# Second layer of a float32 encoder on one core: all heads' probabilities turned through VectorE and DMA, three output blocks in step, the last heads' holds dropped

## The chip, the core and the metric

The kernel runs on one NeuronCore of one Trainium2 chip. The metric is device time in microseconds (us), lower is better. Before the change the median of three runs is 1994.85 us (1994.55 to 1995.7).

## The reference

A two-layer encoder over 256 tokens of width 2048, all in float32. Layer 0 mixes tokens by neighbourhood attention (12 heads of 128), layer 1 by grouped-query attention (12 query heads over 4 key heads, queries and keys normalised per head and rotated by their place in the grid). In both layers 4 more heads attend to 256 memory tokens. The concatenated 16 heads go through one output projection, and a squared-ReLU MLP of width 8192 follows:

```python
z = n @ b_w_in[j]
...
q = axial_rope(rms_norm(split_heads(q, N_MIX_HEADS), b_q_norm[j]))
k = axial_rope(rms_norm(split_heads(k, N_KV_HEADS), b_k_norm[j]))
mix = gqa_block_attention(q, k, split_heads(v, N_KV_HEADS))
...
h = h + jnp.concatenate([mix, cross], axis=-1) @ w_o[i]
n = rms_norm(h, mlp_norm[i])
h = h + jnp.square(jax.nn.relu(n @ w_up[i])) @ w_down[i]
```

Each attention head is `softmax(q k^T / sqrt(128)) v` over 256 keys.

## The kernel before

**Products.** Every float32 operand is split in two parts of a reduced type, `hi` (ScalarE copies, L486) and `lo` (VectorE subtracts, L487), and every product is three matmuls: hi·hi, hi·lo, lo·hi. TensorE does these for the whole run.

**Weights.** Weights come in chunks of 1 MB (a `Work` in `plan`), loaded by DMAs that SyncE issues into three rotating buffers `raw`. A chunk is used in two halves; each half is split into one of four `hi` and one of four `lo` buffers. A buffer comes free when TensorE has used the half that lay in it. A half of an output-projection chunk is 12 matmuls of 128x512. `run_all` walks the halves; each is one tick. `later(n, fn)` runs `fn` n ticks on, so a head's steps are placed by counting ticks; `ahead` of a `Grain` says how many ticks before its matmuls a half is loaded and split. These numbers set when instructions are written; a scheduler then fixes the order of each engine's list, which the engine executes strictly in that order.

**A head in layer 1.** `attention(jobs, at, gap, steps, rest)` places the steps of a block's four heads: the first head's step n at tick `at + steps[n]`, each further head `gap` later.
- `attend`: six score matmuls of 128x256 into `sc_ps`, the negative maximum `nm` on VectorE (L548), two exps on ScalarE (L550) that also sum into `sm`, the reciprocal `rs` (L553), and two multiplications by it on VectorE (L555).
- The probabilities must then be turned, keys onto partitions. The 4 memory heads (12 to 15) and block 0 (heads 0 to 3) do so by `turned`: two VectorE transposes into `sc_t` (L592) that turn inside squares of 32, and four SyncE DMAs into `pT_t` (L597) that carry the squares to their places; `halved` then splits the landed tile into `hi` and `lo` (L486, L487). Blocks 1 and 2 (heads 4 to 11) do it by `attend2`: four TensorE transposes into the PSUM tile `pt_a` (L563), split from there.
- `attend3`: six matmuls of 128x256 on `pT` and the values (`av`, L680 to L682); ScalarE and VectorE split the result into the head's place in `cat`.

**The output projection.** `add_o(1)` takes `cat` in four chunks c of four heads each for four output blocks b: c = 3 holds the memory heads, c = 0, 1, 2 the heads 0 to 3, 4 to 7 and 8 to 11. Before, blocks 0 and 1 run in step: (b, c) = (0,3) (0,0) (1,3) (1,0) (0,1) (1,1) (0,2) (1,2), then block 2's four chunks, then block 3's. The query chunks that make a block's heads are projected just before, so the heads of blocks 1 and 2 run beside these chunks. The sums `ps_m` live in the PSUM pool `acc` (four banks). A second pool `att` (four banks) holds the tiles of heads: `sc_ps`, `pt_a`, `pt_h` (turned queries) and `av`. The last chunks of blocks 0 and 1 are marked `behind` and `last_block`: their splits and matmuls are held behind the steps of heads 10 and 11 by `past` and `issue_after`, and `late_products` writes out their order.

**Layer 0.** `a_k_done` places the steps of the 12 local heads; the last entry of its `steps` is the tick of `attend3_near`, whose `av` matmuls wait for `pT_n`.

## Time and profile before

| what | value |
| --- | --- |
| median of three runs | 1994.85 us |
| the profiled execution | 1995.76 us |
| its span, first to last instruction | 1993.9 us |
| granted TensorE clock, mean | 0.999 |
| busy: TensorE, VectorE, ScalarE | 1984.5, 1715.7, 1327.4 us |
| TensorE instructions of `pt_a` | 32 |

The span is 1.86 us shorter than the execution's time. In rows of groups, the figures behind the count are busy time and the mean duration of one in ns, then idle time of the engine before them and what ended it. In a timeline, a row has its start, its duration, engine, line, operation and tile names, and in brackets the idle time before it. In rows of windows, the window and its length are followed by busy time (and count) of PE, PEld, DVE, ACT and POOL, then the granted clock, the DMA engines' busy share and GB/s. PE is TensorE, DVE VectorE, ACT ScalarE, SP SyncE (SPq its queue).

### The profile page before, as it was taken

Reading aid. Unit: us, or ns where it says so; the run is one execution under the profiler, and the core shown is the slowest. Engines: PE = TensorE matmul, PEld = TensorE weight load, DVE = VectorE, ACT = ScalarE, POOL = GpSimd, SP = SyncE. Lnnn points to the kernel's source line nnn. Section 1 sums busy time; section 2 is a strip of 40 time slices with the busy share of each in tenths; the row PEclk is TensorE's granted clock in tenths of the full one; section 3 lists DMA queues with packets and bytes.
Section 4 is the critical chain, followed back from the end, with each engine's and each line's share of the span. In section 5 each row is a group of like instructions: output and inputs, shape, how many; then the busy total and the mean of one; then the engine's idle time right before and its main releaser. Section 6 shows DMA issues by size and latency. Waiting matters only on the chain.

```text
span 1993.9 us, 32782 instructions
## 1 busy us (share of the span) xinstructions
PE 1984.5 (100%) x12870; PEld 1802.1 (90%) x12870; DVE 1715.7 (86%) x2147; ACT 1327.4 (67%) x1860; POOL 137.4 (7%) x179
## 2 busy tenths in 40 slices
PE   9999999999999999999999999999999999999998
PEld 8999999899999999999998888889999999999997
DVE  6777767589898999999999778778998999999998
ACT  6655555467777767777665657567776777777674
POOL 0000000000000000000000001000000000000000
PEclk9999999999999999999999999999999999999999
DMA  7856655767777777777666764567777777777772
GB/s 293 319 195 201 204 188 185 272 192 241 237 230 231 228 227 237 238 235 227 210 227 210 265 220 153 194 195 256 232 223 239 225 226 238 235 237 228 225 235 106
DMA packets 112731, 446.42 MB, mean 224 GB/s; under 512 B 24128, under 2 KB 45376, under 8 KB 65216
## 3 DMA queue, kind: packets, MB, share of 16 engines
q1 hardware_dynamic: 94560, 413.02, 58.9%
q0 software_dynamic: 17728, 30.78, 9.6%
q8 instruction: 101, 1.65, 0.3%
q14 instruction: 54, 0.44, 0.1%
q10 hardware_dynamic: 288, 0.52, 0.1%
HBM read 397.78 MB, written 4.19 MB: 202 GB/s over the span
## 4 chain that ended last, share of the span: by engine, by line
PE 99%; DMA 0%; issue 0%; ACT 0%; SPq 0%; DVE 0%; DVEq 0%; POOLq 0%; POOL 0%; ACTq 0%
PE ps_u L391 35%; PE ps_s L391 10%; PE p L1185 9%; PE p L1183 9%; PE p L1186 9%; PE ps_m L368 8%; PE ps_m L372 8%; PE ps_m L371 8%; PE sc_ps L544 0%; PE sc_ps L543 0%; PE sc_ps L542 0%; PE av L681 0%; PE av L682 0%; PE av L680 0%; DMA first<-in_mem_rest 0%
## 5 line engine op out<-in xcount | busy, mean ns | idle before, releaser
L391 PE MATMUL ps_u<-hT,uh 128*128 128x256 f32 x3812 | 663.6, 276 | 0.0
L391 PEld LDWEIGHTS ps_u<-hT,uh 128*128 128x128 f32 x3812 | 578.9, 188 | 5.5
L391 PE MATMUL ps_u<-hT,ul 128*128 128x256 f32 x1960 | 541.5, 276 | 0.0
L486 ACT ACTIVATE uh<-raw_U 128x1024 fp32r<-128x1024 f32 x262 | 276.7, 1058 | 207.6 <-PE ps_u L391 194.6
L391 PEld LDWEIGHTS ps_u<-hT,ul 128*128 128x128 f32 x1960 | 368.0, 188 | 0.0
L487 DVE TENSOR_TENSOR ul<-raw_U,uh 128x1024 fp32r<-128x1024 f32 x262 | 318.2, 1218 | 16.6 <-ACT uh L486 15.9
L487 DVE TENSOR_TENSOR lo<-raw,hi 128x1024 fp32r<-128x1024 f32 (+1 forms) x215 | 253.5, 1187 | 87.3 <-ACT hi L486 86.3
L487 DVE TENSOR_TENSOR tl<-t,th 128x2048 fp32r<-128x2048 f32 x116 | 265.5, 2289 | 70.9 <-ACT th L486 70.6
L486 ACT ACTIVATE hi<-raw 128x1024 fp32r<-128x1024 f32 (+1 forms) x215 | 221.2, 1037 | 146.9 <-PE ps_m L372 80.8
L486 ACT ACTIVATE th<-t 128x2048 fp32r<-128x2048 f32 x116 | 222.6, 1919 | 116.9 <-PE p L1186 114.9
L487 DVE TENSOR_TENSOR bl<-b,bh 128x1536 fp32r<-128x1536 f32 x116 | 203.1, 1751 | 0.0
L1183 PE MATMUL p<-th,a_s 128*128 128x512 f32 x464 | 181.2, 391 | 0.0
L1185 PE MATMUL p<-tl,a_s 128*128 128x512 f32 x464 | 181.0, 390 | 0.0
L1186 PE MATMUL p<-th,a_s 128*128 128x512 f32 x464 | 180.5, 389 | 0.0
L1152 POOL DMA_DIRECT2D t<-b x116 | 100.7, 868 | 1144.3 <-ACT t L1151 1060.9
L486 ACT ACTIVATE bh<-b 128x1536 fp32r<-128x1536 f32 x116 | 172.3, 1486 | 7.9
L391 PE MATMUL ps_s<-nT,hi 128*128 128x256 f32 x896 | 154.8, 277 | 0.0
L1186 PE MATMUL p<-bh,a_s 128*128 128x512 f32 x348 | 136.2, 391 | 0.0
L1185 PE MATMUL p<-bl,a_s 128*128 128x512 f32 x348 | 135.7, 390 | 0.0
L1183 PE MATMUL p<-bh,a_s 128*128 128x512 f32 x348 | 135.4, 389 | 0.0
L391 PEld LDWEIGHTS ps_s<-nT,hi 128*128 128x128 f32 x896 | 135.2, 188 | 0.2
L391 PE MATMUL ps_s<-nT,lo 128*128 128x256 f32 x448 | 124.2, 277 | 0.0
(312 smaller groups left out, 3576.6 us busy)
## 6 DMA issues: line engine op xcount, KB each, us to landing
raw_U<-in_w_up SPq DMA_DIRECT2D x128, 1024.0 KB, 5.9
b<-in_w_pair SPq DMA_DIRECT2D x116, 1024.0 KB, 5.7
raw<-in_w_o SPq DMA_DIRECT2D x32, 1024.0 KB, 4.9
t<-b POOLq DMA_DIRECT2D x116, 256.0 KB, 5.1
raw<-in_w_b SPq DMA_DIRECT2D x21, 1024.0 KB, 5.7
raw<-in_w_av SPq DMA_DIRECT2D x12, 1024.0 KB, 5.1
raw<-in_w_aq SPq DMA_DIRECT2D x12, 1024.0 KB, 5.2
raw<-in_w_ak SPq DMA_DIRECT2D x12, 1024.0 KB, 4.8
```

The source lines that it names most:

```text
L368: first = nc.tensor.matmul(ps, ah, hi[:, s], start=st, stop=False)
L371: nc.tensor.matmul(ps, ah, lo[:, s], start=False, stop=False)
L372: final = nc.tensor.matmul(ps, al, hi[:, s], start=False, stop=sp)
L391: ins = nc.tensor.matmul(ps, x, acts[:, k, part], start=k == n == 0, stop=k == KT - 1 and n == 2)
L486: first = nc.scalar.activation(dst_hi, src, AF.Copy)
L487: return first, nc.vector.tensor_tensor(dst_lo, src, dst_hi.bitcast(F32), op=ALU.subtract)
L1152: nc.gpsimd.dma_start(s[:, 3, :], b[:, 1, :], accum_op=ALU.add)
L1183: ins = nc.tensor.matmul(ps, a[:, 0, ai, :], hi[:, s], start=begins, stop=False)
L1185: nc.tensor.matmul(ps, a[:, 0, ai, :], lo[:, s], start=False, stop=False)
L1186: nc.tensor.matmul(ps, a[:, 1, ai, :], hi[:, s], start=False, stop=ends)
```

## The change

All twelve mixer heads of layer 1 now take the way of `turned` and `halved`, with ticks of their own for each block: `at` is 3, 1, 4 for blocks 0, 1, 2, `gap` is 2, 3, 3, and `steps` is (0, 2, 5, 6) for all. In layer 1 the multiplication by `rs` is a ScalarE copy with a scale (L525 in the new file). `add_o(1)` takes blocks 0, 1 and 2 in step, nine chunks ahead of those with c = 2, and block 3 behind them; block 2's two sums take two of the four banks of `att`. The holds of the last heads and `late_products` are gone. In layer 0 the last step of the local heads moves from tick 9 to 8 (every fourth head) and from 5 to 6 (the others). Line numbers behind the removed parts fall: L368, L371, L372 become L340, L343, L344; L486, L487 become L455, L456; L548, L550, L553 become L517, L519, L522; L592, L597 become L564, L569; L680 to L682 become L652 to L654.

```diff
--- before.py
+++ after.py
@@ -81,7 +81,7 @@
     def __init__(self, kind, src, acts, first, begins, last, start, done):
         self.kind, self.src, self.acts = kind, src, acts
         self.first, self.begins, self.last, self.start, self.done = first, begins, last, start, done
-        self.early = self.behind = self.last_block = False
+        self.early = False
 
 
 class Shifted:
@@ -272,15 +272,7 @@
                     tiles["raw"] = pool.tile([P, CH], F32, tag="raw", bufs=bufs, name="raw")
                     box["load"] = nc.sync.dma_start(tiles["raw"], w.src)
             src = tiles["raw"][:, hf * HALF : (hf + 1) * HALF]
-            if w.behind and hf == 1:
-
-                tiles[hf] = new_half(w.kind)
-                past(lambda: box.update(held=split(*tiles[hf], src)), box["pT", NH - 1 if w.last_block else NH - 2])
-            elif plan[plan.index(w) - 1].last_block:
-
-                tiles[hf] = new_half(w.kind)
-                past(lambda: split(*tiles[hf], src), (box["added"],) * 2 if hf else box["cat", NH - 1])
-            elif w.kind == "S" and hf == 0 and plan[plan.index(w) - 1].kind == "M":
+            if w.kind == "S" and hf == 0 and plan[plan.index(w) - 1].kind == "M":
                 tiles[hf] = entered_half(src)
             else:
                 tiles[hf] = new_half(w.kind)
@@ -293,9 +285,6 @@
             if w.kind == "S":
                 s_products(w, hf * (KT // 2), KT // 2, hi, lo)
             else:
-                if w.behind and w.last_block:
-                    late_products(w, hf, hi, lo)
-                    return
                 for i in range(NT):
                     box["late"] = m_products(w, w.first + 2 * hf, 2, i, hi, lo, w.begins and hf == 0,
                                              w.last and hf == 1)
@@ -312,23 +301,6 @@
                     Grain(lambda: run(1), after, None, None, lambda: prep_early(1), far)]
         return [Grain(lambda: run(0), None, None, None, lambda: prep(0)),
                 Grain(lambda: run(1), after, None, None, lambda: prep(1))]
-
-    def late_products(w, hf, hi, lo):
-
-
-        if hf == 0:
-            for i in range(NT):
-                m_products(w, w.first, 1, i, hi, lo, False, False)
-            with tc.issue_after(box["av"].ins):
-                for i in range(NT):
-                    box["between"] = m_products(w, w.first + 1, 1, i, hi[:, 512:], lo[:, 512:], False, False)
-        else:
-            with tc.issue_after(box["av"].ins):
-                for i in range(NT):
-                    m_products(w, w.first + 2, 1, i, hi, lo, False, False)
-            with tc.issue_after(box["late"].ins):
-                for i in range(NT):
-                    m_products(w, w.first + 3, 1, i, hi[:, 512:], lo[:, 512:], False, True)
 
     def new_half(kind):
         s = slice(STILL_AT // 4, STILL_AT // 4 + HALF) if kind == "S" else slice(0, HALF)
@@ -426,9 +398,6 @@
         begin()
         for w in plan[FIRST_CHUNKS:]:
             order.extend([w] if isinstance(w, Grain) else halves_of(w))
-            if isinstance(w, Work) and w.last_block:
-
-                order[-3], order[-2] = order[-2], order[-3]
         reached = [0, 0, 0]
 
         def ahead(n):
@@ -473,7 +442,7 @@
 
             def start(w, b=b, begins=begins):
                 if begins:
-                    pool, tag = (at.att, "att") if banks else (at.acc, "acc")
+                    pool, tag = (at.att, "att") if banks and b in banks else (at.acc, "acc")
                     ps[b] = [pool.tile([P, 512], F32, tag=tag, name="ps_m") for _ in range(NT)]
                 w.ps = ps[b]
 
@@ -552,7 +521,10 @@
         rs = small.tile([P, NT], F32, tag="rs", name="rs")
         box["divided"] = nc.vector.reciprocal(rs, sm)
         for s in range(NT):
-            nc.vector.tensor_scalar(sc[:, s, :], sc[:, s, :], rs[:, s : s + 1], None, op0=ALU.mult)
+            if box["layer"]:
+                nc.scalar.activation(sc[:, s, :], sc[:, s, :], AF.Copy, scale=rs[:, s : s + 1])
+            else:
+                nc.vector.tensor_scalar(sc[:, s, :], sc[:, s, :], rs[:, s : s + 1], None, op0=ALU.mult)
         return sc
 
     def attend2(sc):
@@ -684,10 +656,7 @@
         if by_quarters:
             hi, lo = (x.rearrange("p (t a j) -> p t a j", t=NT, a=4) for x in (hi, lo))
             src = src.rearrange("p (a t j) -> p t a j", t=NT, a=4)
-        if head == NH - 1:
-            past(lambda: box.update({("cat", head): split(hi, lo, src)}), box["held"])
-        else:
-            box["cat", head] = split(hi, lo, src)
+        box["cat", head] = split(hi, lo, src)
 
     def attention(jobs, at, gap=1, steps=(0, 1, 3, 4), rest=0):
 
@@ -703,10 +672,7 @@
             elif bias is not None:
                 return attend3_near(prev, v, head, cat)
             else:
-                if "between" not in box:
-                    return attend3(prev, v, head, cat)
-                with tc.issue_after(box.pop("between").ins):
-                    return attend3(prev, v, head, cat)
+                return attend3(prev, v, head, cat)
             results[n, head] = res
 
         results = {}
@@ -802,7 +768,7 @@
     def add_mem(layer):
         for hd in range(NMH):
             add_s(t[f"w_km{layer}"][hd], get("memT"), km_done(layer, hd), 1 if (layer, hd) == (0, 3) else None)
-        add_m([t[f"w_vm{layer}"][c] for c in range(4)], parts_of("memT"), vm_done(layer), layer == 0)
+        add_m([t[f"w_vm{layer}"][c] for c in range(4)], parts_of("memT"), vm_done(layer), () if layer else (0,))
 
     mem_sq = at.work.tile([P, 512], F32, tag="b_o", bufs=3, name="mem_sq")
 
@@ -880,7 +846,7 @@
             b = at.work.tile([P, NT * NEAR], F32, tag="b_o", bufs=3, name="bias")
             nc.sync.dma_start(b, t["bias"][hd])
             attention([(box.pop(("q", hd)), k, b, head_of(box["v", hd // GH], hd % GH), hd, box["cat"])], 1,
-                      steps=(0, 1, 3, 4 if hd == NH - 1 else 9 if hd % GH == GH - 1 else 5))
+                      steps=(0, 1, 3, 4 if hd == NH - 1 else 8 if hd % GH == GH - 1 else 6))
         return f
 
     def a_qm_done(hd):
@@ -999,16 +965,12 @@
 
     def add_o(layer):
         first, second, third, late = 3, 0, 1, 2
-        for n in (0, 2):
-            if n:
-                order = [(b, c) for b in range(2) for c in range(4)]
-            else:
-                order = [(b, c) for b in range(2) for c in (first, second)]
-                order += [(b, c) for c in (third, late) for b in range(2)]
-            add_ms([([t[f"w_o{layer}"][nb * 4 + c] for c in range(4)], o_done(layer, nb)) for nb in (n, n + 1)],
-                   parts_of("cat"), order)
-            if layer and n == 0:
-                plan[-1].behind = plan[-2].behind = plan[-1].last_block = True
+        early = 2 + layer
+        order = [(b, c) for b in range(early) for c in (first, second)]
+        order += [(b, c) for c in (third, late) for b in range(early)]
+        order += [(b, c) for b in range(early, 4) for c in range(4)]
+        add_ms([([t[f"w_o{layer}"][nb * 4 + c] for c in range(4)], o_done(layer, nb)) for nb in range(4)],
+               parts_of("cat"), order, (2,) if layer else ())
 
 
 
@@ -1520,7 +1482,7 @@
 
     def b_q_done(blk):
         def f(w):
-            outs = normed_heads(w, box["divided"] if blk == 2 else None)
+            outs = normed_heads(w, None)
             qT = at.work.tile([P, 4, 512], F32R, tag="l4", name="qT1")
             if blk == 0:
                 later(1, queries_far, outs)
@@ -1529,8 +1491,7 @@
                 later(1, heads_T, outs, 4, qT)
             kvs = [(blk * 4 + j) // (NH // NKV) for j in range(4)]
             attention([(qT[:, j, :], Far(box["kT"], kv), None, head_of(box["vb"], kv), blk * 4 + j, box["cat"])
-                       for j, kv in enumerate(kvs)], 1 if blk else 3, 2, (0, 3, 6) if blk else (0, 2, 5, 6),
-                      2 if blk == 2 else 0)
+                       for j, kv in enumerate(kvs)], (3, 1, 4)[blk], (2, 3, 3)[blk], (0, 2, 5, 6))
         return f
 
     def b_qm_done(w):
```

## The prediction

> **What bounds the kernel now.** I read the page's busy times and its chain first, then the waits of TensorE, then the windows of the stage that is changed. On the page, line 1 gives busy time and line 4 the chain that ended last.

> ```profile
> span 1993.9 us, 32782 instructions
> ...
> PE 1984.5 (100%) x12870; PEld 1802.1 (90%) x12870; DVE 1715.7 (86%) x2147; ACT 1327.4 (67%) x1860; POOL 137.4 (7%) x179
> ...
> PE 99%; DMA 0%; issue 0%; ACT 0%; SPq 0%; DVE 0%; DVEq 0%; POOLq 0%; POOL 0%; ACTq 0%
> ```

> TensorE is the path from end to end. So an edit gains only what it takes off TensorE, and it loses only where TensorE is made to wait. The view of TensorE's waits shows how few waits there are now:

> ```profile
> PE idle L237 <- POOL mhalf L231: 1.0, 1, 1.0
> PE av L654 <- ACT pT_n L486: 0.5, 1, 0.5
> PE ps_s L391 <- ACT memT L516: 0.3, 1, 0.3
> PE ps_s L391 <- DVE lo L487: 0.2, 1, 0.2
> ```

> That is 2.0 us in all, none of it in the second layer's attention, whose changed heads run between 1200 and 1280 us. The windows of that stage give, after the window's length, the busy time of PE, PEld, DVE, ACT and POOL:

> ```profile
> 1200.00:1220.00 20.00, 20.00 (x98) 16.80 (x96) 19.68 (x41) 13.07 (x32) 0.00 (x0) 1.00 0.60 195
> 1220.00:1240.00 20.00, 20.00 (x109) 17.24 (x108) 17.24 (x33) 15.81 (x42) 3.16 (x4) 1.00 0.52 175
> 1240.00:1260.00 20.00, 20.00 (x117) 17.47 (x116) 15.14 (x29) 11.62 (x25) 0.00 (x0) 1.00 0.31 105
> 1260.00:1280.00 20.00, 20.00 (x118) 17.39 (x117) 12.74 (x29) 9.87 (x25) 0.00 (x0) 1.00 0.27 102
> ```

> TensorE is full in all four, and VectorE and ScalarE each have room in the last two. Nothing on those two engines can be gained; a head whose probabilities come late can be lost.

> **What leaves TensorE.** Eight heads (blocks 1 and 2 of the second layer) no longer turn their probabilities on TensorE: 32 transposes, and nothing else, go from its list. Their group, and one place of them on TensorE's timeline (start, duration; times overlap because matmuls are pipelined, so I read start to start):

> ```profile
> L563 PE MATMUL pt_a<-ident,sc 128*128 128x128 f32 x32 | 5.2, 272 | 0.0
> ```

> ```profile
> 1237.91 0.28 PE L543 MATMUL sc_ps<-kT,qT 128*128 128x256 f32 x1
> 1238.03 0.28 PE L544 MATMUL sc_ps<-kT,qT 128*128 128x256 f32 x1
> 1238.15 0.60 PE L563 MATMUL pt_a<-ident,sc 128*128 128x128 f32 x4
> 1238.50 0.47 PE L368 MATMUL ps_m<-hi,cat 128*128 128x512 f32 x1
> 1238.82 0.39 PE L371 MATMUL ps_m<-lo,cat 128*128 128x512 f32 x1
> 1239.05 0.40 PE L372 MATMUL ps_m<-hi,cat 128*128 128x512 f32 x1
> ```

> Four transposes take 1238.50 − 1238.15 = 0.35 us, and the matmul behind them takes 0.32 to its successor where the next takes 0.23: 0.09 more. So 0.44 for four, 0.11 each, and 32 × 0.11 = **3.5 us** off the path. The bounds are 32 × 0.0875 = 2.8 (no tail) and the group's 5.2 of busy time. In the program before, TensorE's list holds this, where `pt_a` is one head's turned probabilities, `sc_ps` another head's scores and `ps_m` a sum of the output projection:

> ```order
> L543 MATMUL sc_ps_12831<-kT1_11939,qT1_12640 128x256
> L544 MATMUL sc_ps_12831<-kT1_11939,qT1_12640 128x256
> L563 MATMUL pt_a_12868<-ident_112,sc_12768 128x128 x4
> L368 MATMUL ps_m_13200<-hi_13196,cat1_11720 128x512
> L371 MATMUL ps_m_13200<-lo_13197,cat1_11720 128x512
> L372 MATMUL ps_m_13200<-hi_13196,cat1_11720 128x512
> ```

> The row of `pt_a` and its like are gone after the change; the scores are followed directly by the sums.

> [...]

> **What comes instead.** Each of the eight heads now goes exp, scale, two VectorE transposes, four DMAs, two halves of a split. The groups of ScalarE and of VectorE between 1200 and 1290 us (busy, mean ns | idle before) price the steps:

> ```profile
> L486 ACT ACTIVATE hi<-raw 128x1024 fp32r<-128x1024 f32 x26 | 27.3, 1066 | 9.6 <-PE ps_m L372 8.0 <-ACT sc L550 0.7 <-ACT hi L486 0.5
> L550 ACT ACTIVATE sc<-sc_ps,nm 128x256 f32<-128x256 f32 x22 | 10.3, 481 | 3.9 <-DVE nm L548 2.4 <-DVE sc_t L592 1.4
> L486 ACT ACTIVATE cat<-av 128x256 fp32r<-128x256 f32 x12 | 4.7, 391 | 10.1 <-PE av L682 10.1
> L550 ACT ACTIVATION_READ_ACCUMULATOR sc<-sc_ps,nm 128x1 f32 x22 | 4.7, 212 | 0.0
> ...
> L486 ACT ACTIVATE pT_t<-pT_t 128x512 fp32r<-128x512 f32 x4 | 2.5, 631 | 1.4 <-DMA pT_t<-sc_t 1.4
> ```

> ```profile
> L487 DVE TENSOR_TENSOR lo<-raw,hi 128x1024 fp32r<-128x1024 f32 x25 | 30.1, 1219 | 2.9 <-ACT hi L486 2.6
> L555 DVE TENSOR_SCALAR sc<-sc,rs 128x256 f32<-128x256 f32 x24 | 7.2, 348 | 0.2
> L548 DVE TENSOR_REDUCE nm<-sc_ps 128x2 f32<-128x512 f32 x10 | 6.8, 681 | 1.4 <-PE sc_ps L544 1.4
> ...
> L592 DVE STREAM_TRANSPOSE sc_t<-sc 128x256 f32<-128x256 f32 x8 | 4.8, 627 | 0.0
> ...
> L553 DVE RECIPROCAL rs<-sm 128x2 f32<-128x2 f32 x12 | 1.9, 157 | 1.1 <-ACT sc L550 1.0
> ```

> The scale on ScalarE does not occur before in this form. Its bounds are the copy of the same size from PSUM, 0.391, and the exp of the same size, 0.481 with its accumulator's 0.212: 0.39 to 0.69 each. I take 0.39, the copy, since it accumulates nothing. ScalarE gets 32 × 0.39 = 12.5 us more over the layer's 16 heads; VectorE loses 32 × 0.348 = 11.1 and gets 16 × 0.627 = 10.0. Neither engine is on the path by its total.

> The DMAs are priced by two views, SyncE's queue and then ScalarE, which takes the landed tile up:

> ```profile
> 1231.74 2.49 SPq L597 DMA_DIRECT2D pT_t<-sc_t  x4
> ```

> ```profile
> 1218.33 0.64 ACT L486 ACTIVATE pT_t<-pT_t 128x512 fp32r<-128x512 f32 x1 [0.83 <-DMA pT_t<-sc_t]
> ...
> 1235.95 0.63 ACT L486 ACTIVATE pT_t<-pT_t 128x512 fp32r<-128x512 f32 x1 [0.57 <-DMA pT_t<-sc_t]
> ```

> From the first issue to the split's start are 1235.95 − 1231.74 = 4.2 us, of which 2.49 are the four issues, and ScalarE did wait for the landing. Eight heads add 32 issues, 20 us of SyncE's queue; weight loads queue behind them there. They are ordered three tiles ahead, so I put that at nothing; if the cover is gone it costs up to 2.5 us, one head's issues.

> The 0.5 us wait of TensorE in the first layer, for `pT_n`, belongs to the shifted steps of the local attention (9 to 8, 5 to 6): it may go or double, −0.5 to +0.5, and I take nothing. Dropping the holds of the last heads, and the matmuls written out by hand behind them, moves work that TensorE did not wait for: nothing, covered by the full windows above. Taking the third block in step leaves the number of matmuls alone and puts nine weight tiles, not six, ahead of the first use of heads 8 to 11. The last head then has over 5 us to arrive by my count of TensorE's list; nothing there either. Block 2's sums take two of the four banks that scores and results of heads rotate through; a head's scores then wait for the exp of the head two before. I price that at 0 to 0.8 us, and as nothing where the wait below swallows it.

> **Where the new path is late: head 7.** After the change TensorE's list reads as follows. `av_13140` is head 6's result, `sc_ps_13195` head 9's scores, `av_13230` head 7's result, which needs head 7's turned probabilities `pT_t_13100`; `ps_m_13271` is block 2's first sum.

> ```order
> L513 MATMUL sc_ps_13195<-kT1_11939,qT1_12992 128x256
> L343 MATMUL ps_m_13156<-lo_13178,cat1_11720 128x512
> L344 MATMUL ps_m_13156<-hi_13177,cat1_11720 128x512
> L340 MATMUL ps_m_13156<-hi_13177,cat1_11720 128x512
> L343 MATMUL ps_m_13156<-lo_13178,cat1_11720 128x512
> L344 MATMUL ps_m_13156<-hi_13177,cat1_11720 128x512
> L652 MATMUL av_13230<-pT_t_13100,vb_12187 128x256
> L340 MATMUL ps_m_13271<-hi_13214,cat1_11720 128x512
> ```

> Block 2's sums, for which weights are ready, stand behind `av_13230`; TensorE takes its list in order, so they wait with it. On ScalarE the rows that lead there are these: `sc_13044` is head 7, `pT_t_12996` head 6, `hi_13239` and `hi_13267` are weight halves.

> ```order
> L455 ACTIVATE pT_t_12996<-pT_t_12996 128x512
> L455 ACTIVATE hi_13239<-raw_13212 128x1024
> L519 ACTIVATE sc_13044,sm_13046<-sc_ps_13037,nm_13045 128x256 x2
> L455 ACTIVATE cat1_11720<-av_13054 128x256
> L455 ACTIVATE hi_13267<-raw_13265 128x1024
> L525 ACTIVATE sc_13044<-sc_13044,rs_13050 128x256 x2
> ```

> Head 7's exp moved behind the landing of head 6's DMAs, and its scale behind one more weight half. On VectorE its transposes stand behind `lo_13268`, that half's other part, and head 8's maximum:

> ```order
> L456 TENSOR_TENSOR lo_13268<-raw_13265,hi_13267 128x1024
> L517 TENSOR_REDUCE nm_13115<-sc_ps_13107 128x2
> L564 STREAM_TRANSPOSE sc_t_13097<-sc_13044 128x2x4x32 x2
> L456 TENSOR_TENSOR cat1_11720<-av_13140,cat1_11720 128x256
> L517 TENSOR_REDUCE nm_13203<-sc_ps_13195 128x2
> ```

> So the transposes that the probabilities' DMAs wait for come last of the three.

> The wait has a floor. `hi_13267` takes a buffer that TensorE frees at the end of the sums of an earlier half. From there, TensorE has 12 matmuls of 128x512 and 18 of 128x256 until `av_13230`: at the spacings above, 0.2275 (0.23 in the rows) and 0.12, 12 × 0.2275 + 18 × 0.118 = 4.85 us. In the same time the chain needs 1.07 (`hi`) + 1.22 (`lo`) + 0.68 (maximum) + 1.25 (two transposes) + 4.2 (DMAs) + 0.63 (first half of the split) = 9.05. So TensorE waits **at least 4.2 us**.

> The longer chain begins where TensorE frees the buffer of `hi_13177`, which stands ahead of head 6's exp. For head 6: 1.07 + 2 × (0.48 + 0.21) + 0.16 + 0.78 (scale) + 1.25 + 4.2 + 0.63 = 9.5. For head 7 behind it: `hi` 1.07, exp 1.39, the `cat` copy 0.39, `hi` 1.07, `lo` 1.22, maximum 0.68, transposes 1.25, DMAs 4.2, split 0.63 = 11.9. Together 21.4, against 42 matmuls of 128x512, 41 of 128x256 and 8 transposes on TensorE, 15.3: a wait of **6.1 us**. ScalarE overlaps neighbours by about 0.1 each and each change of engine costs a little, so the two about cancel; with DMAs as slow as 0.7 more per head and all hops unhidden it would be 8.3. I take 6.1.

> **What a wait of that length does to the clock.** The end of this trace has one. TensorE's last matmul, and the granted clock (1.00 is full) in two slices after it:

> ```profile
> 1986.40 0.28 PE L372 MATMUL ps_m<-h_p,a_p 128*128 128x256 f32 x1
> ```

> ```profile
> 1991.00:1991.50 0.50, 0.00 (x0) 0.00 (x0) 0.00 (x0) 0.00 (x0) 0.00 (x0) 1.00 1.09 430
> 1991.50:1992.00 0.50, 0.00 (x0) 0.00 (x0) 0.00 (x0) 0.00 (x0) 0.00 (x0) 0.64 0.95 389
> 1992.00:1992.50 0.50, 0.00 (x0) 0.00 (x0) 0.00 (x0) 0.00 (x0) 0.00 (x0) 0.50 0.82 328
> ```

> A mean of 0.64 between 1.00 and 0.50 puts the drop at 1991.64, 4.96 us after the last matmul's end. What a start from cold costs, the run's first matmuls show:

> ```profile
> L237 PE MATMUL idle<-ones x20: 274/421/582, 1.0 to 5.1; 128*128 128x128 f32 x20
> ```

> 19 steps in 4.1 us are 0.216 each, twice the 0.0875 to 0.11 of the 128x128 transposes: half pace for at least 4.1 us, so 2.05 lost. A wait of 6.1 us passes the 4.96 and costs **2.1 us** more; one of 4.2 does not.

> [...]

> **The sum.** The profiled execution took 1995.76 us, 1.9 more than its span and 0.9 more than the median of 1994.85. −3.5 + 6.1 + 2.1 = +4.7, so 2000.5 for that execution and **1999.6** beside the median. A measurement of this kernel can tell 0.2%, 4.0 us, from no change; 1998.9 and more is slower.

> **The rivals.** *The wait stays under the clock's drop.* If head 7's chain runs at its floor of 4.2, the clock holds: −3.5 + 4.2 gives 1995.6, no change. It decides at a wait of 4.96 us; up to there the time ends at 1996.3. [...] For it: the floor counts only what must follow the last release by TensorE. Against it: head 6's landing stands ahead of head 7's exp.

> *No wait: the chain keeps ahead of TensorE.* Then only the 3.5 us count and the time is 1991.3, with the bound of 5.2 even 1989.7, which is faster. This needs the halves ahead of head 7 to be split some 4.2 us earlier than TensorE's freeing allows, or the DMAs to land in under 1 us where 4.2 were measured. For it speaks that no turned head of before made TensorE wait in this layer; against it, that in the windows they lay among fuller work.

> *More heads are late.* Heads 4 to 6 have the same chain with a little more cover. If two of them also lack 1.5 us each, and the weight loads queue behind the 32 added issues for one head's 2.5, the time is 1999.6 + 3 to 5.5, about 2004.

> **How the numbers follow.** Head 7 late with the clock's drop 0.5 (1997.6 to 2003; nine in ten of it above 1998.9), late without it 0.27, no wait 0.13, more heads late 0.1. Slower is then 0.53, nearly all of the first and the last; faster takes a little under half of the no-wait case, 0.06; no change the rest, 0.41. The range leaves out the no-wait case and the tail above 2003: 1994.0 to 2003.0. The likeliest case alone has 1997.6 to 2003.

> **What would show it.** TensorE's waits should hold a row of head 7's result for ScalarE's `pT_t`, 4.2 to 8 us, once, near 1240 us; a granted clock below 1.00 in the 5 us behind it; the group of `pt_a` gone; ScalarE's windows fuller by about 12 us over the layer and VectorE's about level. No such row makes the forecast wrong at its root; a row without a dip of the clock makes it wrong by 2.1; several rows say that the chain is late for all heads.

## The result, and the profile after

The changed kernel takes 1998.8 us (median of 20 runs, 1997.82 to 1999.97), the kernel before 1994.82 in runs beside it: 4.0 us more, a ratio of 1.0019 with a 95% interval of 1.0013 to 1.0026. The interval leaves out 1, and the fastest run of the changed kernel is above the slowest of the kernel before (1996.27), so it is slower, by 0.2%. 1999.6 was forecast.

The page of the changed kernel shows the same chain, TensorE from end to end, with 2.0 us less work on TensorE and 13.8 us more on ScalarE:

```profile
span 1996.8 us, 32815 instructions
...
PE 1982.5 (99%) x12838; PEld 1799.9 (90%) x12838; DVE 1715.6 (86%) x2131; ACT 1341.2 (67%) x1892; POOL 138.3 (7%) x179
...
PE 99%; DMA 0%; issue 0%; ACT 0%; DVE 0%; SPq 0%; DVEq 0%; POOLq 0%; POOL 0%; ACTq 0%
```

TensorE's waits have a new row in first place (total, times, longest, in us). The rows for `pT_n` and `memT` are gone, and one of 0.2 for `hi` is new:

```profile
PE av L652 <- ACT pT_t L455: 5.5, 1, 5.5
PE idle L237 <- POOL mhalf L231: 1.0, 1, 1.0
PE ps_s L363 <- DVE lo L456: 0.2, 1, 0.2
PE ps_s L363 <- ACT hi L455: 0.2, 1, 0.2
```

The windows of the stage, with the granted clock behind the five busy times, put it between 1240 and 1260 us, and the clock dips there:

```profile
1220.00:1240.00 20.00, 20.00 (x108) 17.29 (x108) 18.79 (x38) 16.88 (x53) 2.66 (x4) 1.00 0.51 169
1240.00:1260.00 20.00, 14.50 (x76) 12.28 (x75) 15.06 (x26) 12.98 (x31) 0.00 (x0) 0.84 0.49 150
1260.00:1280.00 20.00, 20.00 (x102) 17.06 (x101) 13.01 (x20) 12.68 (x24) 0.00 (x0) 0.99 0.47 144
```

On TensorE's timeline the wait stands ahead of head 7's first result matmul, and the matmuls of 128x512 behind it come 0.43 us apart, not 0.23, until 1260.3:

```profile
1250.52 0.39 PE L343 MATMUL ps_m<-lo,cat 128*128 128x512 f32 x1
1250.75 0.39 PE L344 MATMUL ps_m<-hi,cat 128*128 128x512 f32 x1
1256.64 0.58 PE L652 MATMUL av<-pT_t,vb 128*128 128x256 f32 x1 [5.50 <-ACT pT_t L455]
1257.02 0.63 PE L340 MATMUL ps_m<-hi,cat 128*128 128x512 f32 x1
1257.44 0.63 PE L343 MATMUL ps_m<-lo,cat 128*128 128x512 f32 x1
...
1260.01 0.51 PE L343 MATMUL ps_m<-lo,cat 128*128 128x512 f32 x1
1260.35 0.39 PE L344 MATMUL ps_m<-hi,cat 128*128 128x512 f32 x1
1260.58 0.40 PE L340 MATMUL ps_m<-hi,cat 128*128 128x512 f32 x1
```

The chain that ended last names what TensorE waited for, step by step (start, duration):

```profile
1250.03 0.68 DVE nm L517
1250.71 1.06 DVE sc_t L564 x2
1251.83 0.54 SPq L569
1252.42 0.60 SPq L569
1253.07 0.59 SPq L569
1253.71 2.14 DMA pT_t<-sc_t
1255.95 0.64 ACT pT_t L455
1256.64 0.58 PE av L652
```

Head 8's maximum, head 7's two transposes, its DMAs, the first half of its split: the end of the chain that the prediction wrote down.

The account closes in the stage. In the profiled executions the second layer's first products of `nT` start at 1085.0 before and 1084.0 after, the MLP's first `ps_u` at 1326.0 and 1328.9: the stage takes 241.0 and 244.9, so 3.9 more. The terms give 5.5 (wait) + 1.8 (half pace from 1256.64 to 1260.24, where the clock rose again) − 3.5 (the forecast for the transposes) = 3.8. Ahead of the stage this pair of executions differs by 1.0 the other way: 0.5 of it in the first 100 us, the rest in the first layer's attention, where this execution of the kernel before waited 0.5 for `pT_n`. Behind the stage both take 667.9 to the end of the span. So the profiled pair shows 2.8 (1998.58 against 1995.76), where the medians show 4.0; the kernel before was profiled in an execution 0.9 above its median, the changed kernel in one 0.2 below.

### The profile page after: what moved, and what is told of

Same layout as the page of the kernel before. It is cut to its first block, busy times and chain, and to the rows that moved or that the text cites. A ratio compares the mean times of both kernels' runs of the same rounds, so it can differ in the third digit from the quotient of the medians.

```text
span 1996.8 us, 32815 instructions
## 1 busy us (share of the span) xinstructions
PE 1982.5 (99%) x12838; PEld 1799.9 (90%) x12838; DVE 1715.6 (86%) x2131; ACT 1341.2 (67%) x1892; POOL 138.3 (7%) x179
## 4 chain that ended last, share of the span: by engine, by line
PE 99%; DMA 0%; issue 0%; ACT 0%; DVE 0%; SPq 0%; DVEq 0%; POOLq 0%; POOL 0%; ACTq 0%
PE ps_u L363 35%; PE ps_s L363 10%; PE p L1147 9%; PE p L1145 9%; PE p L1148 9%; PE ps_m L340 8%; PE ps_m L344 8%; PE ps_m L343 8%; PE av L652 0%; PE sc_ps L513 0%; PE sc_ps L512 0%; PE av L653 0%; PE sc_ps L511 0%; PE av L654 0%; DMA raw<-in_w_first 0%
## 5 line engine op out<-in xcount | busy, mean ns | idle before, releaser
L455 ACT ACTIVATE uh<-raw_U 128x1024 fp32r<-128x1024 f32 x262 | 276.7, 1058 | 206.3 <-PE ps_u L363 193.5
L456 DVE TENSOR_TENSOR lo<-raw,hi 128x1024 fp32r<-128x1024 f32 (+1 forms) x215 | 253.8, 1187 | 95.8 <-ACT hi L455 94.7
L456 DVE TENSOR_TENSOR ul<-raw_U,uh 128x1024 fp32r<-128x1024 f32 x262 | 318.1, 1218 | 16.2 <-ACT uh L455 15.9
L456 DVE TENSOR_TENSOR tl<-t,th 128x2048 fp32r<-128x2048 f32 x116 | 265.5, 2289 | 71.2 <-ACT th L455 70.8
L455 ACT ACTIVATE hi<-raw 128x1024 fp32r<-128x1024 f32 (+1 forms) x215 | 221.5, 1038 | 147.9 <-PE ps_m L344 75.5
L455 ACT ACTIVATE th<-t 128x2048 fp32r<-128x2048 f32 x116 | 222.7, 1919 | 117.2 <-PE p L1148 114.9
L456 DVE TENSOR_TENSOR bl<-b,bh 128x1536 fp32r<-128x1536 f32 x116 | 203.1, 1751 | 0.0
L455 ACT ACTIVATE bh<-b 128x1536 fp32r<-128x1536 f32 x116 | 172.3, 1486 | 7.9
```

The costliest lines, as they stand in the source:

```text
L455: first = nc.scalar.activation(dst_hi, src, AF.Copy)
L456: return first, nc.vector.tensor_tensor(dst_lo, src, dst_hi.bitcast(F32), op=ALU.subtract)
```

## The experiments

Theory A is the prediction's: one late head, 5.5 us of wait and 1.8 of clock, against 3.5 gained. The main rival, B: the added transposes, scales and DMAs load the engines and queues, and head 7 is only where it comes out.

**Head 7's result two ticks later.** One number is added; no work changes.

```diff
-                       for j, kv in enumerate(kvs)], (3, 1, 4)[blk], (2, 3, 3)[blk], (0, 2, 5, 6))
+                       for j, kv in enumerate(kvs)], (3, 1, 4)[blk], (2, 3, 3)[blk], (0, 2, 5, 6),
+                      (0, 2, 0)[blk])
```

> The changed kernel, but the last step of head 7 (its six result matmuls) comes two ticks later; all else is as in the change. Theory A, one late head: the 5.5 us wait of TensorE for head 7 goes, the granted clock stays at 1.00, and only the removed transposes are left: 1998.8 - 5.5 - 1.8 = 1991.5 us, 3.3 under the kernel before. Theory B, the added transposes, scales and DMAs load the other engines and queues: the wait moves to another head and the time stays within 1.5 us of 1998.8.

Measured: 1991.36 us, against 1995.02 before (ratio 0.9981, 0.9973 to 0.9990). In TensorE's waits no row of a head is left, and the window where the dip was is full:

```profile
PE idle L237 <- POOL mhalf L231: 1.0, 1, 1.0
PE ps_s L363 <- DVE lo L456: 0.2, 1, 0.2
PE ps_s L363 <- ACT hi L455: 0.2, 1, 0.2
```

```profile
1240.00:1260.00 20.00, 20.00 (x114) 17.50 (x113) 16.68 (x28) 14.75 (x33) 0.00 (x0) 1.00 0.51 150
```

ScalarE's split of head 7 starts at 1255.85, where it started at 1255.95 in the changed kernel, but TensorE has other work meanwhile; it takes the head up at 1258.42:

```profile
1255.85 0.63 ACT L455 ACTIVATE pT_t<-pT_t 128x512 fp32r<-128x512 f32 x1 [1.38 <-DMA pT_t<-sc_t]
```

```profile
1258.42 0.28 PE L652 MATMUL av<-pT_t,vb 128*128 128x256 f32 x1
```

All added transposes, scales and DMAs are still there: TensorE, VectorE and ScalarE have as many instructions as in the changed kernel (12838, 2131 and 1892). So 7.4 us hang on where six matmuls stand in one list, and B falls as the cause. Of the 7.4, 5.5 are the wait, and 1.9 are left for the clock's dip (1.8 by the trace). This version is faster than both kernels.

**First layer's steps back.** `8 if hd % GH == GH - 1 else 6` is `9 … else 5` again.

```diff
-                      steps=(0, 1, 3, 4 if hd == NH - 1 else 8 if hd % GH == GH - 1 else 6))
+                      steps=(0, 1, 3, 4 if hd == NH - 1 else 9 if hd % GH == GH - 1 else 5))
```

> The changed kernel with the first layer's local heads at their old steps (9 and 5). Theory A: the 0.5 us wait of TensorE for pT_n comes back and nothing else: 1999.3 us (1998.8 to 1999.5). If the shifted steps had saved more, or lost, the time is below 1998.3 or above 1999.8.

Measured: 1998.89 us, 0.1 from the changed kernel: no measurable difference. The time lies in the range of A, but not for A's reason: the wait for `pT_n`, gone in the changed kernel's profile, did not come back in this one, so these steps alone do not decide it. Head 7's wait stays, as long as before:

```profile
1256.92 0.58 PE L652 MATMUL av<-pT_t,vb 128*128 128x256 f32 x1 [5.52 <-ACT pT_t L455]
```

The clock, though, falls only at about 1256.48 here and is back at about 1259.88, so TensorE loses (1259.88 − 1256.92) / 2 = 1.5 us to it, not 1.8. The last section comes back to this.

**Scale back on VectorE.**

```diff
-            if box["layer"]:
-                nc.scalar.activation(sc[:, s, :], sc[:, s, :], AF.Copy, scale=rs[:, s : s + 1])
-            else:
-                nc.vector.tensor_scalar(sc[:, s, :], sc[:, s, :], rs[:, s : s + 1], None, op0=ALU.mult)
+            nc.vector.tensor_scalar(sc[:, s, :], sc[:, s, :], rs[:, s : s + 1], None, op0=ALU.mult)
```

> The changed kernel with the scale of the second layer's probabilities back on VectorE (32 instructions of 0.348 us instead of 32 of 0.39 to 0.45 on ScalarE). Theory A: the chain of a turned head is as long as before, but VectorE, which also holds the transposes and the lo halves, runs later: heads 6 and 7 both make TensorE wait, 8 to 12 us in all with one or two dips of the clock: 2001 to 2006 us. Theory C, ScalarE's new scale is what made head 7 late: the wait falls below 2 us and the time to 1993 or less.

Measured: 2005.84 us (ratio to before 1.0055, 1.0042 to 1.0069). The profiled execution was the slowest of the five (2008.69). Its TensorE timeline has three waits for turned heads, 10.3 us in all, where two were expected:

```profile
1246.17 0.39 PE L649 MATMUL av<-pT_t,vb 128*128 128x256 f32 x1 [1.70 <-ACT pT_t L455]
1257.66 0.58 PE L649 MATMUL av<-pT_t,vb 128*128 128x256 f32 x1 [3.02 <-ACT pT_t L455]
1266.18 0.58 PE L649 MATMUL av<-pT_t,vb 128*128 128x256 f32 x1 [5.59 <-ACT pT_t L455]
```

The matmuls behind the three waits lose another 5.7 us at half pace (1.71, 1.47 and 2.57). Theory C falls: the scale on ScalarE is not what made head 7 late; with the scale on VectorE more heads are late. One reason stands in VectorE's timeline, where a weight half's `lo` now comes between a head's two transposes:

```profile
1236.78 0.62 DVE L524 TENSOR_SCALAR sc<-sc,rs 128x256 f32<-128x256 f32 x2
1237.30 0.63 DVE L561 STREAM_TRANSPOSE sc_t<-sc 128x256 f32<-128x256 f32 x1
1237.85 1.18 DVE L456 TENSOR_TENSOR lo<-raw,hi 128x1024 fp32r<-128x1024 f32 x1
1238.95 0.63 DVE L561 STREAM_TRANSPOSE sc_t<-sc 128x256 f32<-128x256 f32 x1
```

How much of the three waits comes from that, and how much from the rest of the new order, these runs don't separate.

**Transposes back on TensorE for heads 4 to 11.**

```diff
-…, (3, 1, 4)[blk], (2, 3, 3)[blk], (0, 2, 5, 6))
+…, (3, 1, 4)[blk], (2, 3, 3)[blk], (0, 3, 6) if blk else (0, 2, 5, 6))
```

> The changed kernel, but heads 4 to 11 turn their probabilities on TensorE again (32 transposes, steps 0, 3, 6), with the three blocks in step, the scale on ScalarE and the holds gone. Theory A: the 3.5 us of transposes come back and the wait for head 7 shrinks by the DMAs' 4.2 us to 0 to 2.5 us without a dip of the clock: 1994.3 to 1996.8 us. Theory D, three blocks in step or the shared banks are what costs: the time stays at 1998 or more with waits at ps_m or sc_ps.

Measured: 1996.46 us (ratio 1.0008, 0.9999 to 1.0017): within the range of A. One wait is left in the stage, and the clock holds at 1.00:

```profile
PE av L652 <- DVE cat L456: 1.1, 1, 1.1
```

It is not the expected one for head 7's probabilities. It is a head's first result matmul, held by VectorE's split of another head's result. That matmul reads no `cat`; what the split gives it, by the program, is the bank of `att` that it read out. So the shared banks do cost something in this order, 1.1 us, more than the 0 to 0.8 that the prediction gave them. All that is left of the change without the new way of turning comes to 1.4 us here, this wait included, and the interval does not exclude zero; D falls as the cause of the 4.0.

**The wait filled with idle matmuls.**

```diff
+        if box["layer"] and head == 7:
+            for _ in range(24):
+                nc.tensor.matmul(av[:, SEQ : SEQ + P], ones, ones, start=True, stop=True)
```

> The changed kernel with 24 added matmuls of 128x128 (of a tile of ones, into a part of head 7's bank that nothing reads) written just ahead of head 7's result, about 24 x 0.21 = 5.1 us of work in place of the 5.5 us wait. Theory A, the wait costs 5.5 us and the clock's dip 1.8 more: the clock stays at 1.00 and the time falls although work is added, to 1998.8 - 1.8 - 0.4 = 1996.6 us (1995.8 to 1997.3). Theory E, the dip costs nothing that is not given back: 1998.3 us or more.

Measured: 1996.75 us, 2.05 below the changed kernel, with 5.3 us of work added (start of the filling to the start of the next matmul; the trace records two matmuls for each of the 24):

```profile
1250.32 5.52 PE L651 MATMUL av<-ones 128*128 128x128 f32 x48
1255.60 0.47 PE L343 MATMUL ps_m<-lo,cat 128*128 128x512 f32 x1
```

```profile
1240.00:1260.00 20.00, 20.00 (x133) 18.00 (x132) 16.32 (x29) 13.84 (x32) 0.00 (x0) 1.00 0.39 108
```

The clock stayed at 1.00. The filling does not stand in for the wait alone: block 2's first sums also came ahead of head 7's result in this list, so TensorE had real work from 1255.60 on, and took that head up at 1259.58. So the run is better read as the first experiment with 5.3 us of work added: 1991.36 + 5.3 = 1996.7, as measured. The changed kernel has 5.5 of wait in place of the 5.3, which is 0.2 more; the other 1.85 are the dip. E falls.

**Heads 4 to 7 two ticks apart.**

```diff
-…, (3, 1, 4)[blk], (2, 3, 3)[blk], (0, 2, 5, 6))
+…, (3, 1, 4)[blk], (2, 2, 3)[blk], (0, 2, 5, 6))
```

> The changed kernel with heads 4 to 7 two ticks apart instead of three; nothing else. Theory A: head 7's exp and scale are written earlier, ahead of the weight halves that it stood behind, and the wait goes or stays under 1.2 us with no dip of the clock: 1991.3 to 1992.8 us. Theory B, a turned head must be given more ticks, not fewer: heads 5 to 7 wait and the time is 1996 or more.

Measured: 1992.64 us (ratio 0.9986, 0.9977 to 0.9995), with one wait of 0.6 us in the stage, for a `cat` half, and no dip (the clock is 1.00 from 1220 to 1300). Another way to have head 7 in time gives nearly the same time. It is 1.3 above the first; 0.6 of that is the wait, 0.2 the difference between the kernel before's medians beside the two (1995.22 and 1995.02), and the rest was not traced.

**Turned heads alone, two blocks in step.** Both start from the kernel before, with steps (0, 2, 5, 6) for all blocks; the first also has the scale on ScalarE.

```diff
-                       for j, kv in enumerate(kvs)], 1 if blk else 3, 2, (0, 3, 6) if blk else (0, 2, 5, 6),
+                       for j, kv in enumerate(kvs)], 1 if blk else 3, 2, (0, 2, 5, 6),
```

> The kernel before (two blocks in step, holds of the last heads kept) with only heads 4 to 11 turned on VectorE and the layer's scale on ScalarE. Theory A, three blocks in step are what gives the last heads time: heads 9 and 11 now make TensorE wait, 3 to 8 us in all, with or without a dip of the clock: 1994.8 - 3.5 + 3 to 10 = 1994.3 to 2001 us. Theory F, the blocks in step are not needed: no wait and 1991.5 us.

> As the kernel before with only heads 4 to 11 turned on VectorE, scale left on VectorE, two blocks in step. Theory A: VectorE, which is 97% busy around 1200 to 1220 us already, gets 10 us of transposes: waits of 8 to 14 us in several places, with dips of the clock: 2000 to 2008 us. Theory F: within 2 us of the run with the scale on ScalarE.

Measured: 1995.03 us with the scale on ScalarE (ratio 1.0000, 0.9991 to 1.0009), 2000.68 with it on VectorE (1.0027, 1.0017 to 1.0037). The waits of the first:

```profile
PE ps_m L368 <- ACT cat L486: 1.2, 1, 1.2
PE av L683 <- ACT pT_t L486: 1.0, 2, 0.8
PE idle L237 <- POOL mhalf L231: 1.0, 1, 1.0
PE av L684 <- DVE pT_t L487: 0.7, 2, 0.3
```

2.9 us of waits, just under the 3 expected, take back most of the 3.5, and F falls. They are five short waits, for two turned heads and for a half of `cat`, and the clock stays at 1.00. The run with the scale on VectorE has 7.3 us of waits in the layer, a little under the 8 to 14 expected, and a granted clock of 0.91 in the window from 1260 to 1280, 1.00 in the others from 1220 to 1300. Its largest waits:

```profile
PE av L680 <- ACT pT_t L486: 3.9, 2, 3.0
PE ps_m L368 <- ACT cat L486: 2.2, 3, 1.1
```

So turning the heads on VectorE, with the scale on ScalarE and nothing else, gains nothing that can be measured; with the rest of the change and head 7 two ticks later it gains 3.7. What that rest is worth by its parts (three blocks in step, the ticks of each block, the dropped holds) these runs don't separate, and other ticks with two blocks in step were not tried. The scale on ScalarE earns its place in both orders: 5.7 us here, 7.0 in the order of the change. What spoilt the change was one head's place in it.

## Why the prediction was right, and where it was not

**The sign and the mechanism** held: one wait, for head 7's `pT_t`, at the place named, and the clock's dip behind it.

**The transposes**: 3.5 us forecast, 3.7 measured by the first experiment against before (3.6 in the stage of the two traces). TensorE is full in the stage in both, at a clock of 1.00, and it has 32 matmuls fewer (12838 against 12870), the transposes, so the difference is theirs.

**The wait**: 6.1 forecast, floor 4.2; it was 5.5. The floor's chain, from `hi_13267` to the split's end, took 8.8 (1247.79 to 1256.58) where 9.05 was written:

```profile
1247.79 1.06 ACT L455 ACTIVATE hi<-raw 128x1024 fp32r<-128x1024 f32 x1
1248.75 0.90 ACT L525 ACTIVATE sc<-sc,rs 128x256 f32<-128x256 f32 x2
```

It began about 1.6 us after TensorE had freed the buffer (1246.23, the end of the matmul that stands 30 ahead of the wait, by the prediction's count), since ScalarE still had head 7's exps ahead of it, as the longer chain says. That chain was too long by 1.1 from head 6's landing on, 11.4 (1245.15 to 1256.58) against 12.5 with that head's split: ScalarE and VectorE overlap neighbours by about 0.1 (`hi` above ends at 1248.85, the scales start at 1248.75; head 8's maximum ends at 1250.71, the transposes start at 1250.63), and there the changes of engine do not make that up, as had been assumed. The forecast was only 0.6 too long, so what lies ahead of that landing took about 0.5 more than written: two errors that partly cancel, which is luck.

**The clock**: 2.1 forecast, 1.8 measured. But the step "a wait of 6.1 us passes the 4.96" was wrong as a rule. The clock fell 2.3 us after the last matmul here, and in the run with the scale on VectorE after a wait of 1.7. So the rival with 4.96 as its deciding point had no such point, and by the estimate of the last section the chance of 0.27 for a late head without the dip was too high. That the size came so close is partly luck as well: with the first layer's steps back, a wait of the same length lost 1.5.

**Costs put at nothing.** The weight loads behind the added DMAs on SyncE, the shared banks and the dropped holds cost nothing that the first experiment shows; the banks' 1.1 us came only with the transposes back on TensorE. The first layer's steps make no difference that can be measured (0.1). The scale on ScalarE was mis-sized, 0.52 each in a group's mean where 0.39 was taken, inside the bounds:

```profile
L525 ACT ACTIVATE sc<-sc,rs 128x256 f32<-128x256 f32 x24 | 11.1, 518 | 3.5 <-DVE rs L522 3.5
```

It mattered little: a pair takes 0.90, 0.1 over the 0.78 that the chain was given. What it is worth against VectorE was not asked in the prediction at all, and its 7.0 us are nearly as much as the late head's 7.4.

## What to carry to other kernels

When TensorE is full, read the changed order for the longest stretch in which other engines' instructions stand with few matmuls between them, and look for a wait there first; an estimate of its length is the dependent chain less the matmuls ahead of it. In these runs the dip behind a wait of 5.5 or 5.6 us cost another 1.5 to 2.6. Moving independent matmuls ahead of the one that waits took both away here, 7.4 us, without a shorter chain. Before judging a change by its time, try each late place alone; here one number turned 1.0019 into 0.9981.

## What the runs showed of the hardware

```profile
1247.00:1247.50 0.50, 0.50 (x5) 0.50 (x5) 0.40 (x1) 0.34 (x2) 0.00 (x0) 0.92 0.09 24
1247.50:1248.00 0.50, 0.50 (x4) 0.50 (x3) 0.50 (x1) 0.42 (x1) 0.00 (x0) 0.50 0.00 0
...
1250.50:1251.00 0.50, 0.50 (x3) 0.31 (x2) 0.50 (x3) 0.25 (x1) 0.00 (x0) 0.66 0.94 393
...
1257.50:1258.00 0.50, 0.34 (x1) 0.34 (x2) 0.36 (x1) 0.50 (x4) 0.00 (x0) 0.66 0.45 115
...
1261.00:1261.50 0.50, 0.00 (x0) 0.00 (x0) 0.50 (x3) 0.11 (x2) 0.00 (x0) 0.92 0.00 0
...
1264.00:1264.50 0.50, 0.00 (x0) 0.00 (x0) 0.50 (x2) 0.00 (x0) 0.00 (x0) 0.99 0.49 110
...
1271.00:1272.00 1.00, 1.00 (x8) 0.86 (x7) 0.33 (x1) 0.91 (x2) 0.00 (x0) 0.84 0.00 0
```

Fall 1247.42, rise 1250.84, fall 1257.66, rise 1261.08, fall 1264.49, rise 1271.32: distances of 3.42, 6.82, 3.42, 3.41 and 6.83 us. In the changed kernel half-microsecond windows of 0.92 and 0.76 put the fall at 1253.42 and the rise at 1260.24, 6.82 apart. In the run with the first layer's steps back there are windows of 2 us, and they put the two at about 1256.48 and 1259.88, 3.40 apart:

```profile
1256.00:1258.00 2.00, 1.08 (x3) 0.98 (x4) 1.10 (x2) 1.43 (x3) 0.00 (x0) 0.62 0.75 262
1258.00:1260.00 2.00, 2.00 (x6) 1.52 (x6) 0.67 (x2) 0.00 (x0) 0.00 (x0) 0.53 0.93 325
```

The table has TensorE's idle time in the 3.41 us that end at each fall, and for two of the falls in the 3.41 us ahead of those:

| the 3.41 us that end at | idle in them, us | the clock then |
| --- | --- | --- |
| 1247.42, scale on VectorE | 1.70 | fell, after TensorE had gone on |
| 1257.66, scale on VectorE | 3.02 | fell |
| 1264.49, scale on VectorE | all | fell |
| 1253.42, changed kernel | 2.28 | fell |
| 1253.07, first layer's steps back | 1.67 | stayed |
| 1256.48, first layer's steps back | all | fell |
| 1988.23, kernel before, its end | 1.55 | stayed |
| 1991.64, kernel before, its end | all | fell |

The rise at 1261.08 came with TensorE already idle again for 0.5. A wait of 1.1 us (transposes back on TensorE) left the clock at 1.00, and so did five short ones of 2.9 together (turned heads, two blocks in step). No limit is read from the table: its 1.70 and 1.67 differ by about what the readings allow, since a mean of two digits over 2 us gives a time to 0.02 us, and the ends of matmuls are modelled in the profile.

The prediction's 4.96 is then the time of one case, not a threshold. The fall came 2.28 us after the last matmul in the changed kernel and 5.07 with the first layer's steps back, and these two waits of one length, 5.50 and 5.52 us, lost 1.8 and 1.5. Waits of 1.70 and 3.02 us, shorter than the prediction's floor of 4.2, had dips behind them. That a wait at the floor would have brought the dip too is an estimate from those two; no run had a wait of that length.
